# First MLP chunk by plain products, the activation sums of the seven-product scheme formed behind it, and the last modulation group in the merge

## The chip, the core and the metric

The kernel runs on one core of a Trainium2 chip. The metric is the device time of one launch in microseconds: the median of the runs. The kernel before takes 1075.11 us, the median of 3 runs from 1074.37 to 1075.24.

## What is computed

One trunk layer of a diffusion backbone, for 512 latent tokens and 128 context tokens, 640 in all, with 1024 features. A modulation vector comes from a product of the conditioning with `w_ada` (six groups of 1024 columns: shift, scale and gate for the mixer and for the MLP). The mixer joins two branches with sigmoid gates (called the merge here) and multiplies by `w_out`. Then comes the MLP, with a hidden width of 4096.

```python
shift1, scale1, gate1, shift2, scale2, gate2 = jnp.split(mod, N_MOD, axis=-1)
h = rmsnorm(x, pre1) * (1 + scale1) + shift1
mix = ((g_a * y_mlstm + g_b * y_attn) @ w_out)      # the merge, then the output product
x = x + gate1 * rmsnorm(mix, post1)
h = rmsnorm(x, pre2) * (1 + scale2) + shift2
ff = jnp.square(jax.nn.relu(h @ w_mlp1)) @ w_mlp2
x = x + gate2 * rmsnorm(ff, post2)
```

All of it is float32. A product of two float32 matrices is made of three products in a shorter format: each operand is split into a high and a low part, and high by high, high by low and low by high are summed (`mm3`, lines 116 to 118, or the inner loop of `product`, line 942).

## The kernel before

A TileContext takes the program in the order in which it is written, orders each engine's instructions with a simulated timeline (`schedule_with_timeline_sim`), and adds the waits. So an instruction written later can stand earlier on its engine where the simulation finds it ready. Within an engine the order is then fixed. `tc.issue_after(x)` puts the instructions of a block behind `x` on `x`'s engine.

**The merge** (lines 775 to 816) runs over eight blocks j of 128 features. Each takes 144 matmuls of 320 columns for two gates and two branch outputs. `ada_rest` (line 739) is a generator of eight modulation groups: each loads four pieces of `w_ada2` (512 KB each), makes one group of rows with 16 matmul instructions (`ada_rows`, line 149), and turns them with four transposes (line 155). One group is written ahead of the loop and one in each of j = 0 to 5. The eighth, cb = 7 (the second half of the MLP's gate), has a pool of its own (`own_pool`, line 737), is loaded through SP's queue and is written at line 980, after the output stage.

**The output stage** (lines 873 to 966) runs over five tiles of 128 tokens. `out_tile` has three parts: 48 matmuls of 512 columns into two banks; then the norm, the gate and the residual (the sum x2, line 895, which is also stored), and the second norm (lines 898 to 903); then eight transposes (line 907) into two banks and the modulation on ACT and VectorE (lines 911 and 914), which writes that tile's columns of `h2`. The transposes of tile t stand behind the matmuls of tile t+1. The eight `w_out` pieces take all eight units of the weight ring. PSUM is eight single banks here (line 921).

**The MLP** runs over eight chunks of 512 hidden columns, each made of two pairs of 256. A pair's product over 1024 features and 640 tokens is cut in two along hidden columns, features and tokens, and takes seven products in the place of eight, each of 12 matmuls of 320 columns. The seven need sums and differences of the activation's quarters, `S3` to `S7`, formed once from `h2` (lines 995 to 1018), and of the weights' quarters (`factors`, line 842: four subtractions on GpSimd, then high and low parts by `quarters` on ACT and VectorE). The quarters are `A(i, j)`, with tokens i and features j. `f2[1]` and `f2[2]` are the high and low parts of `A(0,0)` and `A(0,1)`, formed at tile 3 (lines 965 and 966). `squared` (line 1022) makes relu squared of each product and splits it. Then `sums` (line 1123) makes ten products of `w_mlp2`, 12 matmuls of 512 columns each, into `acc`, on chunk 0 with a copy (line 1140). `acc` takes the memory of `h2`.

In chunk 0 the two first products of each pair (`first_two`, line 947), which need `f2[1]` and `f2[2]` alone, are written ahead of the last tile's transposes. The other ten products of the two pairs alternate (line 1085), after `S3` to `S7`. `prime` (line 945) opens a bank with a product that counts for nothing, so that a copied partial sum can be added to.

Of the kernel before, what the change touches and what calls it, by code (L numbers as in the profile page):

```python
# [6 lines left out]
F32 = mybir.dt.float32  # L7
# [5 lines left out]
P = 128  # L13
NT = 5
TOK = 640
KD = 8
# [10 lines left out]
def _build(ctx, tc, nc, a, dbg):  # L27
# [44 lines left out]
    def bank2():  # L72
        return psum[2][1].tile([P, 1024], F32, name="b2")

    def bank1():
        return psum[1][1].tile([P, 512], F32, name="b1")
# [657 lines left out]
        pT.__exit__(None, None, None)  # L734
    dbg("aT", aT)

    own_pool = {}

    def ada_rest(pY):
        for cb in range(8):  # L740
            pY = own_pool.get(cb, pY)
            raws = []
            for u in range(4):
                raw = pY.tile([P, 2, 512], F32, name="aw2", bufs=3 if cb > 6 else 2)
                (nc.sync if cb > 6 else G).dma_start(raw, a["w_ada2"][cb * 4 + u].rearrange("p (k n) -> p k n", k=2))  # L745
# [27 lines left out]
    with pool("pY", side="right") as pY:  # L773
# [25 lines left out]
        for j in range(KD):  # L799
            sgs = []  # L800
            wy = [x.rearrange("p (q k n) -> p q k n", q=2, k=4) for x in load_w(a["w_y"][j])]
            for q in range(2):
                w = [x.rearrange("p (k n) -> p k n", k=8) for x in load_w(a["w_g"][q * 8 + j])]
                pg = halves(bank2())
                mode_b(pg, w, h1, KD)
                sg = pY.tile([P, TOK], F32, name=f"sg{q}", bufs=2)
                s3 = sg.rearrange("p (h n) -> p h n", h=2)
                S.activation(out=s3, in_=pg[:, :, 0:320], func=AF.Sigmoid)
                py = halves(bank2())
                mode_b(py, (wy[0][:, q], wy[1][:, q]), ys[q], 4)  # L810
                V.tensor_tensor(out=s3, in0=s3, in1=py[:, :, 0:320], op=ALU.mult)  # L811
                sgs.append(sg)
            V.tensor_tensor(out=sgs[0], in0=sgs[0], in1=sgs[1], op=ALU.add)
            S.copy(zh[:, j, :], sgs[0])
            V.tensor_tensor(out=zl[:, j, :], in0=sgs[0], in1=zh[:, j, :], op=ALU.subtract)
            next(ada, None) if j < 6 else None
    dbg("zh", zh); dbg("zl", zl)
    pO.__exit__(None, None, None)
    pN.__exit__(None, None, None)
# [53 lines left out]
    def out_tile(t):  # L873
# [28 lines left out]
        else:  # L902
            V.tensor_scalar(out=mix, in0=x2, scalar1=r, scalar2=None, op0=ALU.mult)
        yield
        pt = [bank1(), bank1()]
        for k in range(KD):
            mark["turn"] = T.transpose(pt[k // 4][:, k % 4 * 128:(k % 4 + 1) * 128], mix[:, k * 128:(k + 1) * 128], ident).ins
        for b in (1, 0):
            for k in range(4 * b, 4 * b + 4):
                if b:  # L910
                    S.activation(out=h2[:, k, c], in_=pt[1][:, k % 4 * 128:(k % 4 + 1) * 128], func=AF.Identity,
                                 scale=modA[1][:, k, gi:gi + 1], bias=modB[1][:, k, gi:gi + 1])
                else:
                    V.tensor_scalar(out=h2[:, k, c], in0=pt[0][:, k * 128:(k + 1) * 128], scalar1=modA[1][:, k, gi:gi + 1],
                                    scalar2=modB[1][:, k, gi:gi + 1], op0=ALU.mult, op1=ALU.add)
        yield

    weights(3, keep=1)
    pAd = pool("pAd", side="right")
    own_pool[7] = pAd.__enter__()  # L920
    banks(0, 8)
    wo = [tuple(x.rearrange("p (k n) -> p k n", k=2) for x in load_w(a["w_out"][u])) for u in range(8)]
    xs = {}

# [19 lines left out]

    def prime(b):
        T.matmul(b, f2[1][0][:, 0, 0:128], f2[1][0][:, 0, :], start=True, stop=True)
    def first_two(f, bX, bY):
        product(bX, f[1], f2[1], True)
        prime(bY)
        S.copy(bY, bX)  # L950
        product(bX, f[2], f2[2], False)

    behind = []
    for t in range(NT):
        if t >= 3:
# [6 lines left out]
        if t == 3:  # L962
            for j in range(2):
                f2[1 + j] = sub[:, 2 * j], sub[:, 2 * j + 1]
                S.copy(sub[:, 2 * j], A(0, j))
                V.tensor_tensor(out=sub[:, 2 * j + 1], in0=A(0, j), in1=sub[:, 2 * j], op=ALU.subtract)

    fs = [{}, {}]
    for n in range(2):
        raw = pW_.tile([P, 1024], F32, name="raw", bufs=2)  # L970
        nc.sync.dma_start(raw, a["w_mlp1"][2 * n])
        fs[n][1], fs[n][2] = quarters(raw)
    bs = [bank1()[:, 0:320] for _ in range(2)]
    first_two(fs[0], *bs)
    rests = [factors(*raw_pair(a["w_mlp1"][0:2]), fs[0])]
    bs += [bank1()[:, 0:320] for _ in range(2)]
    first_two(fs[1], *bs[2:])
    next(behind[-1])
    with tc.issue_after(mark["load"]):
        next(ada)  # L980
    next(ada, None)
    pZ.__exit__(None, None, None)
    pAd.__exit__(None, None, None)
    weights(0, keep=1)
    weights(1, keep=1)
    dbg("h2", h2)


# [3 lines left out]
    pH = pool("pH", side="left")  # L992
    pH_ = pH.__enter__()

    s1 = [pW_.tile([P, 1024], F32, name="raw", bufs=2)[:, 0:640].rearrange("p (k n) -> p k n", k=2) for _ in range(2)]
    ks = (slice(0, 2), slice(2, 4))
    fac = {i: [pH_.tile([P, 4, 320], F32R, name=f"S{i}" + s) for s in "hl"] for i in (3, 4, 7, 6, 5)}

# [2 lines left out]
        mark[f"S{i}"] = S.copy(hi, x).ins  # L1001
        V.tensor_tensor(out=lo, in0=x, in1=hi, op=ALU.subtract)

    for h, k in enumerate(ks):
        V.tensor_tensor(out=s1[h], in0=A(1, 0)[:, k, :], in1=A(1, 1)[:, k, :], op=ALU.add)
        parts(5, h, s1[h])
    for h, k in enumerate(ks):
        mark["S2"] = G.tensor_tensor(out=s1[h], in0=s1[h], in1=A(0, 0)[:, k, :], op=ALU.subtract).ins
        parts(6, h, s1[h])
    for h, k in enumerate(ks):  # L1010
        G.tensor_tensor(out=A(1, 0)[:, k, :], in0=A(0, 0)[:, k, :], in1=A(1, 0)[:, k, :], op=ALU.subtract)
        parts(7, h, A(1, 0)[:, k, :])
    for h, k in enumerate(ks):
        V.tensor_tensor(out=A(0, 1)[:, k, :], in0=A(0, 1)[:, k, :], in1=s1[h], op=ALU.subtract)
        parts(3, h, A(0, 1)[:, k, :])
    for h, k in enumerate(ks):
        parts(4, h, A(1, 1)[:, k, :])
    f2.update(fac)
    acc = pA_.tile([P, NT, 1024], F32, name="h1h")
    ssm = small.tile([P, NT, 4], F32, name="ssm", bufs=1)  # L1020

# [51 lines left out]
    for ch in range(NCH):  # L1073
        us = []
        if ch == 0:
            uu = [u_pair() for _ in range(2)]
            bs += [bank1()[:, 0:320] for _ in range(4)]
            for b in bs[6:]:
                prime(b)
# [5 lines left out]
            two = [pair(fs[i], True, uu[i], [bs[n] for n in b_]) for i, b_ in enumerate(((0, 4, 1, 6, 7), (2, 5, 3, 0, 4)))]  # L1085
            for i in (0, 0, 1, 0, 1, 0, 1, 0, 1, 1):
                next(two[i])
            us = [(u[0][n], u[1][n]) for u in uu for n in range(2)]
        else:
            if ch == 1:  # L1090
                banks(0, 5)
                pfork = tc.tile_pool(name="pfork", bufs=1, space=bass.MemoryType.PSUM, reuse_waits="tile")
                pfork_ = pfork.__enter__()
                forks = [pfork_.tile([P, 512], F32, name="b" + s)[:, 0:320] for s in "YWV"]

                for b in forks:
                    prime(b)
            for p in range(2):
                n = ch * 2 + p
                f = {}  # L1100
                factors(*raw_pair(a["w_mlp1"][2 * n:2 * n + 2]), f)()
# [4 lines left out]
        if ch == NCH - 1:  # L1106
# [7 lines left out]
        ws = [[load_w(a["w_mlp2"][ch, nh, m]) for m in range(2)] for nh in range(2)]  # L1114
# [149 lines left out]
```

## Time and profile before

| | us |
|---|---|
| median of the runs | 1075.11 |
| the profiled execution, its own time | 1075.53 |
| its span | 1073.6 |
| TensorE busy | 1025.3 |
| VectorE busy | 572.8 |
| ACT busy | 428.5 |
| GpSimd busy | 247.6 |
| last matmul of the output stage starts at | 612.01 |
| first product of chunk 1 starts at | 697.70 |

The table is read by stage: the merge ends at about 552 us, the output stage at 612 us, chunk 0 at 697 us, and seven more chunks follow. Matmuls overlap, so a matmul's own duration is longer than its share of the time. What counts is the distance from one start to the next.

### The profile page before, as it was taken

The numbers are of one execution on the slowest core, as the hardware profiler recorded it, in microseconds if no ns is written. First come the engines' busy times: TensorE is split into PE (matmuls) and PEld (weight loads), VectorE is DVE, ScalarE is ACT, GpSimd is POOL, SyncE is SP. The second block draws the span as 40 slices with busy tenths as digits, with TensorE's granted clock in tenths as the row PEclk, the third lists the DMA queues.
The fourth block names the chain that finished last, engine by engine and source line by source line (L and its number), as shares of the span: only waits on it lengthen the run. The fifth ranks groups of instructions, "written<-read, shape, count | busy, mean of one in ns | idle before, by whom it ended". The sixth has DMA issues, their size and how long they took to land.

```text
span 1073.6 us, 15721 instructions
## 1 busy us (share of the span) xinstructions
PE 1025.3 (96%) x6322; PEld 909.4 (85%) x6322; DVE 572.8 (53%) x963; ACT 428.5 (40%) x788; POOL 247.6 (23%) x222
## 2 busy tenths in 40 slices
PE   4999999899999999999999947999999999999997
PEld 2899899888789888888997837798989898989896
DVE  3655255577663223333343589465656566565557
ACT  4354243277775222222233554442424242424242
POOL 3011235424560000010000074222131314040201
PEclk9999999999999999999999977999999999999999
DMA  9444142111002444444355134222223131313034
GB/s 373 157 132 142 40 119 68 66 41 40 21 2 79 137 137 138 152 145 157 100 178 213 40 118 151 85 79 79 84 74 96 63 111 47 118 40 119 1 103 171
DMA packets 40408, 113.06 MB, mean 105 GB/s; under 512 B 4312, under 2 KB 14200, under 8 KB 39056
## 3 DMA queue, kind: packets, MB, share of 16 engines
q1 hardware_dynamic: 35520, 96.06, 26.4%
q0 software_dynamic: 4096, 14.70, 4.3%
q10 hardware_dynamic: 720, 1.31, 0.3%
q8 instruction: 49, 0.80, 0.3%
q14 instruction: 23, 0.19, 0.1%
HBM read 106.08 MB, written 5.98 MB: 104 GB/s over the span
## 4 chain that ended last, share of the span: by engine, by line
PE 89%; DVE 4%; POOL 2%; issue 2%; ACT 2%; DMA 1%; SPq 0%; POOLq 0%; DVEq 0%; ACTq 0%
PE b L116 19%; PE b L118 19%; PE b L117 19%; PE b L942 9%; PE bY L942 5%; PE b L149 3%; PE bV L942 2%; PE bW L942 2%; PE b L695 2%; PE b L229 2%; PE b L683 1%; PE b L470 1%; PE b L472 1%; PE b L496 1%; DMA x<-x 1%
## 5 line engine op out<-in xcount | busy, mean ns | idle before, releaser
L112 DVE TENSOR_TENSOR wl<-raw,wh 128x1024 fp32r<-128x1024 f32 (+2 forms) x64 | 77.7, 1215 | 163.3 <-ACT wh L111 163.3
L111 ACT CAST wh<-raw 128x1024 fp32r<-128x1024 f32 (+2 forms) x66 | 66.7, 1011 | 172.3 <-PE b L117 155.1
L117 PE MATMUL b<-h1l,wh 128*128 128x320 f32 x384 | 120.1, 313 | 0.0
L116 PE MATMUL b<-h1h,wh 128*128 128x320 f32 x384 | 119.8, 312 | 0.0
L118 PE MATMUL b<-h1h,wl 128*128 128x320 f32 x384 | 118.8, 309 | 0.0
L848 POOL TENSOR_TENSOR x<-gate 128x512 f32<-128x512 f32 x16 | 22.0, 1376 | 253.4 <-DMA gate<-w_mlp 250.4
L116 PEld LDWEIGHTS b<-h1h,wh 128*128 128x128 f32 x384 | 72.2, 188 | 6.3 <-DVE sg L811 4.2
L117 PEld LDWEIGHTS b<-h1l,wh 128*128 128x128 f32 x384 | 72.2, 188 | 6.0 <-issue 6.0
L118 PEld LDWEIGHTS b<-h1h,wl 128*128 128x128 f32 x384 | 72.2, 188 | 0.2 <-issue 0.2
L117 PE MATMUL b<-wlx,uh 128*128 128x512 f32 (+1 forms) x174 | 67.6, 389 | 0.0
L116 PE MATMUL b<-whx,uh 128*128 128x512 f32 (+1 forms) x174 | 66.9, 391 | 0.0
L1142 DVE TENSOR_TENSOR h1h<-h1h,b 128x512 f32<-128x512 f32 (+1 forms) x71 | 46.2, 672 | 37.0 <-PE b L118 36.8
L118 PE MATMUL b<-whx,ul 128*128 128x512 f32 (+1 forms) x174 | 64.3, 390 | 0.0
L117 PE MATMUL b<-wl,uh 128*128 128x512 f32 x150 | 59.1, 394 | 0.0
L1031 ACT CAST uh<-u 128x320 fp32r<-128x320 f32 x64 | 29.3, 459 | 72.6 <-DVE u L1028 41.5
L116 PE MATMUL b<-wh,uh 128*128 128x512 f32 x150 | 57.8, 396 | 0.0
L118 PE MATMUL b<-wh,ul 128*128 128x512 f32 x150 | 56.6, 395 | 0.0
L745 POOL DMA_DIRECT2D aw<-w_ada x28 | 15.2, 546 | 162.9 <-PE b L149 155.7
L612 POOL TENSOR_TENSOR pt<-pt,sm 128x640 f32<-128x640 f32 x32 | 40.0, 1255 | 46.9 <-DVE sm L610 44.6
L112 DVE TENSOR_TENSOR wlx<-raw,whx 128x1024 fp32r<-128x1024 f32 (+2 forms) x27 | 32.3, 1196 | 28.8 <-ACT whx L111 28.7
L149 PE MATMUL b<-aw,csil 128*32 128x256 f32 (+1 forms) x256 | 35.4, 526 | 9.1 <-DMA aw<-w_ada 9.1
L1032 DVE TENSOR_TENSOR ul<-u,uh 128x320 fp32r<-128x320 f32 x64 | 32.5, 509 | 13.6 <-ACT uh L1031 12.7
(443 smaller groups left out, 2852.8 us busy)
## 6 DMA issues: line engine op xcount, KB each, us to landing
raw<-w_mlp SPq DMA_DIRECT2D x34, 512.0 KB, 3.2
gate<-w_mlp SPq DMA_DIRECT2D x32, 512.0 KB, 4.7
aw<-w_ada POOLq DMA_DIRECT2D x28, 512.0 KB, 4.1
aw<-w_ada SPq DMA_DIRECT2D x8, 1024.0 KB, 12.0
raw<-w_g SPq DMA_DIRECT2D x16, 512.0 KB, 5.4
x<-x SPq DMA_DIRECT2D x10, 512.0 KB, 7.9
raw<-w_y SPq DMA_DIRECT2D x8, 512.0 KB, 3.4
raw<-w_out SPq DMA_DIRECT2D x8, 512.0 KB, 3.6
```

The source lines that it names most:

```text
L111: S.copy(hi, raw)
L112: eng.tensor_tensor(out=lo, in0=raw, in1=hi, op=ALU.subtract)
L116: T.matmul(out, lh, rh, start=start, stop=False)
L117: T.matmul(out, lh, rl, start=False, stop=False)
L118: T.matmul(out, ll, rh, start=False, stop=stop)
L149: T.matmul(ps[32 * j:32 * j + 32, 0:n], csil[:, k, :], raws[k], start=k < 4, stop=k >= 4, tile_position=(0, 32 * j))
L612: G.tensor_tensor(out=pt, in0=pt, in1=sm.broadcast_to([P, 640]), op=ALU.mult)
L848: G.tensor_tensor(out=t13[:, 0:512], in0=q2[0], in1=q1[0], op=ALU.subtract)
L942: T.matmul(out, w[u][:, k, :], x[v][:, k, :], start=start and k == 0 and i == 0, stop=k == 3 and i == 2, skip_group_check=True)
L1031: S.copy(uh[:, c], u)
L1032: V.tensor_tensor(out=ul[:, c], in0=u, in1=uh[:, c], op=ALU.subtract)
L1142: V.tensor_tensor(out=o, in0=o, in1=ps, op=ALU.add)
```

## The change

- The last modulation group goes back into the merge, at j = 6, through GpSimd's queue like the others, and its pool goes away.
- The output stage has four single banks and two double banks in the place of eight single ones; the transposes use the double ones.
- Chunk 0 multiplies four blocks of 128 hidden columns (`w0`, four loads) by both halves of the tokens, with 24 matmuls each. The first token half uses `f2[1]` and `f2[2]`, the second plain high and low parts of `A(1,0)` and `A(1,1)`, kept in the tiles `S3` and `S4`. The fourth block stands behind the last transposes on TensorE.
- `S5`, `S6`, `S7` and then the true `S3` are written behind these products. Their buffers `s1` are now those named `mix`.
- The extra weight unit comes at chunk 1, not ahead of chunk 0. Chunk 1's first factors stand behind the last `S2` subtraction on GpSimd, and chunk 0's `w_mlp2` pieces behind the last tile's modulation on ACT and VectorE.

```diff
-                raw = pY.tile([P, 2, 512], F32, name="aw2", bufs=3 if cb > 6 else 2)
-                (nc.sync if cb > 6 else G).dma_start(raw, a["w_ada2"][cb * 4 + u]...)
+                raw = pY.tile([P, 2, 512], F32, name="aw2", bufs=2)
+                G.dma_start(raw, a["w_ada2"][cb * 4 + u]...)
...
-            next(ada, None) if j < 6 else None
+            next(ada, None)
...
-        pt = [bank1(), bank1()]
+        pt = [bank2(), bank2()]
...
-    banks(0, 8)
+    banks(2, 4, (1, 2))
...
-    fs = [{}, {}]
-    for n in range(2):
-        raw = pW_.tile([P, 1024], F32, name="raw", bufs=2)
-        nc.sync.dma_start(raw, a["w_mlp1"][2 * n])
-        fs[n][1], fs[n][2] = quarters(raw)
-    bs = [bank1()[:, 0:320] for _ in range(2)]
-    first_two(fs[0], *bs)
-    rests = [factors(*raw_pair(a["w_mlp1"][0:2]), fs[0])]
-    bs += [bank1()[:, 0:320] for _ in range(2)]
-    first_two(fs[1], *bs[2:])
+    w0 = []
+    for m in range(4):
+        with tc.issue_after(mark["x2"]) if m == 3 else ExitStack():
+            w0.append([x.rearrange("p (k n) -> p k n", k=8) for x in load_w(a["w_mlp1"][m])])
+    pZ.__exit__(None, None, None)
+    weights(0, keep=1)
     next(behind[-1])
-    with tc.issue_after(mark["load"]):
-        next(ada)
-    next(ada, None)
...
+    for h in range(2):
+        parts(3, h, A(1, 0)[:, ks[h], :])
+    for h in range(2):
+        parts(4, h, A(1, 1)[:, ks[h], :])
...
         if ch == 0:
             uu = [u_pair() for _ in range(2)]
-            rests[0]()
-            with tc.issue_after(mark["S2"]), tc.issue_after(mark["S5"]):
-                rests.append(factors(*raw_pair(a["w_mlp1"][2:4]), fs[1]))
-            rests[1]()
-            two = [pair(fs[i], True, uu[i], ...) for i, b_ in enumerate(...)]
-            for i in (0, 0, 1, 0, 1, 0, 1, 0, 1, 1):
-                next(two[i])
             us = [(u[0][n], u[1][n]) for u in uu for n in range(2)]
+            for hf in range(2):
+                q = (f2[1], f2[2]) if hf == 0 else (f2[3], f2[4])
+                for m in range(CH):
+                    ps = bank1()[:, 0:320]
+                    with tc.issue_after(mark["turn"]) if m == 3 and hf == 0 else ExitStack():
+                        for k in range(KD):
+                            x = [y[:, k % 4, :] for y in q[k // 4]]
+                            mm3(ps, w0[m][0][:, k, :], w0[m][1][:, k, :], *x, k == 0, k == KD - 1)
+                    squared(*us[m], hf, ps=ps)
+            for h, k in enumerate(ks):                 # S5, S6, S7, true S3: moved here from ahead of chunk 0
+                V.tensor_tensor(out=s1[h], in0=A(1, 0)[:, k, :], in1=A(1, 1)[:, k, :], op=ALU.add)
+                parts(5, h, s1[h])
...
+            for h, k in enumerate(ks):
+                V.tensor_tensor(out=A(0, 1)[:, k, :], in0=A(0, 1)[:, k, :], in1=s1[h], op=ALU.subtract)
+                parts(3, h, A(0, 1)[:, k, :])
         else:
             if ch == 1:
+                weights(1, keep=1)
...
+                with tc.issue_after(mark["S2"]) if n == 2 else ExitStack():
+                    rest = factors(*raw_pair(a["w_mlp1"][2 * n:2 * n + 2]), f)
+                rest()
...
+        with tc.issue_after(mark["h2s"]) if ch == 0 else ExitStack(), tc.issue_after(mark["h2v"]) if ch == 0 else ExitStack():
+            ws = [[load_w(a["w_mlp2"][ch, nh, m]) for m in range(2)] for nh in range(2)]
```

## Rows read from the trace of the kernel before

**Rows 1.** The page: TensorE's busy tenths and its granted clock, in 40 equal slices.

```profile
PE   4999999899999999999999947999999999999997
PEclk9999999999999999999999977999999999999999
```

**Rows 2.** Busy time by stretch: length, PE, PEld, DVE, ACT, POOL, clock, DMA share.

```profile
622.00:635.00 13.00, 4.12 (x21) 1.25 (x20) 11.73 (x14) 8.00 (x14) 10.70 (x6) 0.75 0.48 159
635.00:656.00 21.00, 10.58 (x38) 9.29 (x39) 19.05 (x20) 7.61 (x11) 12.55 (x7) 0.59 0.17 59
656.00:697.80 41.80, 41.41 (x211) 35.51 (x210) 24.06 (x28) 19.42 (x32) 14.48 (x10) 1.00 0.35 122
697.80:750.50 52.70, 52.70 (x290) 47.23 (x289) 31.21 (x44) 18.40 (x30) 12.31 (x8) 1.00 0.25 80
```

**Rows 3.** TensorE's waits between 612 and 700 us: total, times, longest.

```profile
PE b L762 <- DVE gcol L758: 5.6, 1, 5.6
PE b L942 <- ACT wh L832: 5.0, 1, 5.0
PE b L942 <- DVE S6l L1002: 3.3, 1, 3.3
PE b L149 <- DMA aw<-w_ada: 2.8, 1, 2.8
```

**Rows 4.** TensorE's timeline: start, own duration, line, operands; idle before and its releaser.

```profile
575.94 1.09 PE L907 MATMUL b<-cst,mix 128*128 128x128 f32 x8 [1.82 <-ACT mix L901]
...
612.01 0.40 PE L118 MATMUL b<-whx,zl 128*128 128x512 f32 x1
612.62 1.09 PE L907 MATMUL b<-cst,mix 128*128 128x128 f32 x8 [0.21 <-ACT mix L901]
613.47 0.54 PE L942 MATMUL b<-h1l,whx 128*128 128x320 f32 x2
...
653.01 0.47 PE L942 MATMUL b<-S6h,wh 128*128 128x320 f32 x1
653.27 0.47 PE L942 MATMUL b<-S6l,wh 128*128 128x320 f32 x1
...
697.70 0.45 PE L942 MATMUL b<-h1l,wh 128*128 128x320 f32 x2
```

**Rows 5.** The chain that ended last, one product of chunk 1: start, length, what.

```profile
708.13 1.76 PE bY L942 x12
```

**Rows 6.** The merge blocks j = 6 and 7: length, TensorE busy, clock, DMA share, GB/s.

```profile
505.51:530.60 25.09, 25.09 (x166) 1.00 0.30 104
530.60:552.00 21.40, 21.40 (x147) 1.00 0.39 125
```

**Rows 7.** VectorE's timeline around the last tile and the sums, columns as in rows 4.

```profile
609.48 1.22 DVE L833 TENSOR_TENSOR wlx<-raw,whx 128x1024 fp32r<-128x1024 f32 x1
...
619.80 0.49 DVE L1028 TENSOR_TENSOR u<-u 128x320 f32<-128x320 f32 x1 [0.30 <-ACT u L1027]
620.21 0.75 DVE L903 TENSOR_SCALAR mix<-x,rs_x 128x1024 f32<-128x1024 f32 x1
...
626.34 3.70 DVE L1005 TENSOR_TENSOR raw<-h1h 128x640 f32<-128x640 f32 x2
...
642.35 3.69 DVE L1002 TENSOR_TENSOR S4l<-h1h,S4h 128x640 fp32r<-128x640 f32 x2
...
653.18 0.81 DVE L1002 TENSOR_TENSOR S3l<-h1h,S3h 128x640 fp32r<-128x640 f32 x1
```

**Rows 8.** GpSimd's timeline at the sums, columns as in rows 4.

```profile
629.32 4.59 POOL L1011 TENSOR_TENSOR h1h<-h1h 128x640 f32<-128x640 f32 x2
636.78 4.96 POOL L1008 TENSOR_TENSOR raw<-raw,h1h 128x640 f32<-128x640 f32 x2
641.71 1.84 POOL L848 TENSOR_TENSOR x<-gate 128x512 f32<-128x512 f32 x1
```

**Rows 9.** DMA issues of 590 to 700 us: count, KB each, median us to landing.

```profile
raw<-w_mlp SPq DMA_DIRECT2D x6, 512.0 KB, 3.3
```

More of the change, by code (lines that the diff above doesn't have):

```diff
@@ L735, in _build @@
     dbg("aT", aT)
-    own_pool = {}
     def ada_rest(pY):
         for cb in range(8):
-            pY = own_pool.get(cb, pY)
             raws = []
             for u in range(4):
-                raw = pY.tile([P, 2, 512], F32, name="aw2", bufs=3 if cb > 6 else 2)
-                (nc.sync if cb > 6 else G).dma_start(raw, a["w_ada2"][cb * 4 + u].rearrange("p (k n) -> p k n", k=2))
+                raw = pY.tile([P, 2, 512], F32, name="aw2", bufs=2)
+                G.dma_start(raw, a["w_ada2"][cb * 4 + u].rearrange("p (k n) -> p k n", k=2))
                 raws += [raw[:, 0, :], raw[:, 1, :]]
@@ L910, in out_tile @@
                 if b:
-                    S.activation(out=h2[:, k, c], in_=pt[1][:, k % 4 * 128:(k % 4 + 1) * 128], func=AF.Identity,
-                                 scale=modA[1][:, k, gi:gi + 1], bias=modB[1][:, k, gi:gi + 1])
-                else:
-                    V.tensor_scalar(out=h2[:, k, c], in0=pt[0][:, k * 128:(k + 1) * 128], scalar1=modA[1][:, k, gi:gi + 1],
-                                    scalar2=modB[1][:, k, gi:gi + 1], op0=ALU.mult, op1=ALU.add)
+                    mark["h2s"] = S.activation(out=h2[:, k, c], in_=pt[1][:, k % 4 * 128:(k % 4 + 1) * 128], func=AF.Identity,
+                                               scale=modA[1][:, k, gi:gi + 1], bias=modB[1][:, k, gi:gi + 1]).ins
+                else:
+                    mark["h2v"] = V.tensor_scalar(out=h2[:, k, c], in0=pt[0][:, k * 128:(k + 1) * 128], scalar1=modA[1][:, k, gi:gi + 1],
+                                                  scalar2=modB[1][:, k, gi:gi + 1], op0=ALU.mult, op1=ALU.add).ins
         yield
     weights(3, keep=1)
-    pAd = pool("pAd", side="right")
-    own_pool[7] = pAd.__enter__()
-    banks(0, 8)
+    banks(2, 4, (1, 2))
     wo = [tuple(x.rearrange("p (k n) -> p k n", k=2) for x in load_w(a["w_out"][u])) for u in range(8)]
@@ L946, in prime @@
         T.matmul(b, f2[1][0][:, 0, 0:128], f2[1][0][:, 0, :], start=True, stop=True)
[L947 to L951, printed above, removed]
     behind = []
@@ L993, in _build @@
     pH_ = pH.__enter__()
-    s1 = [pW_.tile([P, 1024], F32, name="raw", bufs=2)[:, 0:640].rearrange("p (k n) -> p k n", k=2) for _ in range(2)]
+    s1 = [pR_.tile([P, 1024], F32, name="mix", bufs=2)[:, 0:640].rearrange("p (k n) -> p k n", k=2) for _ in range(2)]
     ks = (slice(0, 2), slice(2, 4))
@@ L1002, in parts @@
         V.tensor_tensor(out=lo, in0=x, in1=hi, op=ALU.subtract)
[L1004 to L1017, printed above, removed]
     f2.update(fac)
+    for h in range(2):
+        parts(3, h, A(1, 0)[:, ks[h], :])
+    for h in range(2):
+        parts(4, h, A(1, 1)[:, ks[h], :])
     acc = pA_.tile([P, NT, 1024], F32, name="h1h")
@@ L1076, in _build @@
             uu = [u_pair() for _ in range(2)]
-            bs += [bank1()[:, 0:320] for _ in range(4)]
-            for b in bs[6:]:
-                prime(b)
-            rests[0]()
-            with tc.issue_after(mark["S2"]), tc.issue_after(mark["S5"]):
-                rests.append(factors(*raw_pair(a["w_mlp1"][2:4]), fs[1]))
-            rests[1]()
-            two = [pair(fs[i], True, uu[i], [bs[n] for n in b_]) for i, b_ in enumerate(((0, 4, 1, 6, 7), (2, 5, 3, 0, 4)))]
-            for i in (0, 0, 1, 0, 1, 0, 1, 0, 1, 1):
-                next(two[i])
-            us = [(u[0][n], u[1][n]) for u in uu for n in range(2)]
+            us = [(u[0][n], u[1][n]) for u in uu for n in range(2)]
+            for hf in range(2):
[11 more added lines that the diff above has]
+            for h, k in enumerate(ks):
+                mark["S2"] = G.tensor_tensor(out=s1[h], in0=s1[h], in1=A(0, 0)[:, k, :], op=ALU.subtract).ins
+                parts(6, h, s1[h])
+            for h, k in enumerate(ks):
+                G.tensor_tensor(out=A(1, 0)[:, k, :], in0=A(0, 0)[:, k, :], in1=A(1, 0)[:, k, :], op=ALU.subtract)
+                parts(7, h, A(1, 0)[:, k, :])
+            for h, k in enumerate(ks):
+                V.tensor_tensor(out=A(0, 1)[:, k, :], in0=A(0, 1)[:, k, :], in1=s1[h], op=ALU.subtract)
+                parts(3, h, A(0, 1)[:, k, :])
         else:
             if ch == 1:
+                weights(1, keep=1)
                 banks(0, 5)
@@ L1100, in _build @@
                 f = {}
-                factors(*raw_pair(a["w_mlp1"][2 * n:2 * n + 2]), f)()
+                with tc.issue_after(mark["S2"]) if n == 2 else ExitStack():
+                    rest = factors(*raw_pair(a["w_mlp1"][2 * n:2 * n + 2]), f)
+                rest()
                 u = u_pair()
@@ L1113, in _build @@
                 nc.sync.dma_start(x2[:, t, :], a["scratch_x2"][t])
-        ws = [[load_w(a["w_mlp2"][ch, nh, m]) for m in range(2)] for nh in range(2)]
+        with tc.issue_after(mark["h2s"]) if ch == 0 else ExitStack(), tc.issue_after(mark["h2v"]) if ch == 0 else ExitStack():
+            ws = [[load_w(a["w_mlp2"][ch, nh, m]) for m in range(2)] for nh in range(2)]
         last = ch == NCH - 1
```

4 lines of the change are left out of this document (removed).

## The prediction

> **What bounds the kernel now.** The page's slices come first: TensorE is at nine tenths or more almost everywhere, so a stage's time is its matmuls, and there is one hole, in two slices near 620 to 660 us, where the granted clock falls as well [rows 1]. The stretches give its size. From 622 to 656 us, 34.0 us, TensorE is busy for 14.7 and idle for 19.3 us, and its granted clock is 0.75 and then 0.59; the stretches behind are full at a clock of 1.00 [rows 2]. The waits say why: a modulation group's chain (5.6 us for `gcol`, 2.8 us for its last load), a weight factor (5.0 us) and the parts of an activation sum (3.3 us) [rows 3]. The timeline gives the ends: the last output matmul starts at 612.01, the first product of chunk 1 at 697.70 [rows 4].
>
> The hole is thus the work between `h2` and the products that need its sums. VectorE runs the first sum at 626.34 and the last split of the sums at 653.18 [rows 7], 27.6 us in all with that split, and in this time only a few products can run.
>
> **Prices.** Twelve matmuls of 320 columns take 1.76 us at the full clock [rows 5], 0.1467 us each. At 653 us starts are 0.26 us apart [rows 4], the lower of the two clocks, so a matmul then costs about 0.12 us more. A chunk in the steady state takes 52.70 us [rows 2], of which 14 x 1.76 = 24.64 are the seven-product part; the other 28.06 are 120 matmuls of 512 columns, 0.234 each. Eight transposes take 613.47 - 612.62 = 0.85 us [rows 4].
>
> **Chunk 0, before.** From the end of the output matmuls, 612.01 + 0.234 = 612.24, to 697.70 are 85.46 us [rows 4].
>
> **Chunk 0, after, with no wait added.** Tile 3's transposes with the wait ahead of them stay as they are: 613.47 - 612.24 = 1.23 us [rows 4]. Tile 4's add 0.85. The plain products are 4 blocks x 2 halves x 24 = 192 matmuls in the place of 168: 28.2 us, so the change pays 3.5 us in work. The `w_mlp2` part is 28.06 us. Three primes of chunk 1 are 0.44 us; the four others go, and lay in the hole. The sum is 58.8 us, 26.7 less than before.
>
> **The moved modulation group.** In the merge TensorE is full, so here it is paid in whole. A group written at the end of one block runs in the next. Block j = 6, which holds such a group, takes 25.09 us, and j = 7, which holds none, 21.40 [rows 6]: 3.7 us. By the matmuls of a block, 144 x 0.1467 = 21.1, it is 4.0, which I take. Its four loads leave SP's queue, where one stood behind the last `x2` store, and go to GpSimd's, as for the six groups before; in the block of [rows 6] that holds the last of those, TensorE was busy for 25.09 of 25.09 us, so I cost the queue at nothing. If that cover failed, a group would cost what its last load cost in the hole, 2.8 us [rows 3]. `gcol`, its transpose and the store of the gate row follow in the merge, and nobody needs them before the last chunk.
>
> So far the gain is 26.7 - 4.0 = 22.7 us.
>
> **Waits that the change may add**, none of them in the trace of before:
>
> - The third and fourth weight pieces. There are two raw buffers. The second is read until 609.48 + 1.22 = 610.7 [rows 7]; a load lands in 3.3 us [rows 9], cast and split take about 1.1 and 1.22, so a piece is there at about 616.5. The third block starts at 613.47 + 2 x 3.52 = 620.5. The fourth piece's split is ordered behind the `x2` sum, and queued on VectorE behind it is only the scaling of tile 4 at 620.21 [rows 7], while its block starts at 625. Between 0 and 1.2 us (one split late): 0.6.
> - The plain `S3` and `S4`. Tile 4's scaling ends at 620.96 [rows 7], so its transposes fit behind the third block, at 624.0, and end at 624.9. Modulation (some 1.4 us, as in the timeline of the four operations) and one cast of 0.7 and one split of 0.81 [rows 7] put the first parts at about 628; the first half's fourth block ends at 628.4. The four splits in a row end at about 631, and `S4` is first read at 630.2. With two squares of 0.49 + 0.49 [rows 7] and a weight split ahead of them it would be 4 us later. Between 0 and 4: 1.0.
> - `acc` over `h2`. The products end at 628.4 + 14.1 + about 1 = 643.5. `acc` may not be written before the last sum is formed from `h2`; with four banks, four of the ten sums, 2.81 us each, can run without it, until 654.7. The chain from 629 needs 27.6 us if it is as slow as before, so 656.6: 1.9 us late. But before it shared its engines with two pairs' factors; with splits at 0.81 us and nothing between, it ends near 646, when TensorE leaves the old `S3`. The far end is in the rivals. Between 0 and 1.9 here: 0.8.
> - Chunk 1's factors: two units of weights come free only late in chunk 0's `w_mlp2` part, after its seventh sum, about 8 us ahead of chunk 1, and two casts and two splits of about 1.1 and 1.22 each follow. Between 0 and 2.8 (as if one load were late): 0.3.
>
> Together 2.7 us. A wait of this size does not move the clock here: after the 1.82 us ahead of tile 0's transposes [rows 4] the slices stay at nine tenths or more [rows 1].
>
> **Weight against the trace.** The sums move to a time when GpSimd forms chunk 1's factors. Beside GpSimd a VectorE split took 1.85 us (`S4l`), and without it 0.81 (`S3l`) [rows 7]. In the Trainium skill, "SBUF — State Buffer", section "Who interferes with whom", only the port pair that VectorE and GpSimd share causes contention, as an exclusive lock; a VectorE instruction with two SBUF inputs contends with a GpSimd one that reads SBUF. The slow split agrees with it; that it would make GpSimd's and VectorE's times add up here is the first rival, and the time would be 1066.
>
> **The rivals.**
>
> 1. *The sums come late.* VectorE's work from 625: 16 sums and splits of 0.81, eight squares of 0.98, four weight splits of 1.22, 1.4 of modulation: 27 us, to 652. GpSimd's: 4.96 + 4.59 + four factor steps of 1.84 [rows 8] = 16.9. If each instruction holds the other engine up, the chain ends near 669 and TensorE waits 14 us for `acc`; half of that is likelier, since in 635 to 656 us the two were busy for 19.05 + 12.55 in 21.0 us [rows 2]. Time: 1058.5 to 1067.
> 2. *Tile 4's transposes stand too early on TensorE.* They are written ahead of the plain products, and only the fourth block is bound to stand behind them. If the simulated order puts them first, TensorE idles from 613.5 to 621.0: 7.5 us, and some 25 matmuls at the lower clock cost 3 more. Time: about 1066. Against it: before, VectorE took chunk 0's square at 619.80, ahead of tile 4's scaling that is written earlier [rows 7], so the order follows readiness.
> 3. *Slower.* If the order on VectorE puts the sums behind the second half's squares, chunk 0's `w_mlp2` splits and chunk 1's factors, the chain begins at 644, plus seven weight splits of 1.22, and at 27.6 us ends at 680; TensorE waits for `acc` from 654.7, 25 us, and comes back at the lower clock, some 40 matmuls at 0.12 = 4.8. That is 30 + 1.9 against 22.7: about 1085. It decides from a chain that ends after 671. For it speaks that GpSimd and ACT steps of the chain wait for each other; against it the same row of readiness [rows 7].
> 4. *The change does not do what it says: the hole only moves*, to the second half's start, which waits for the plain `S3` and `S4` as the sums' products waited before. To eat the gain that wait must be about 22 us, so ACT and VectorE would have to take other work first. Against it: the last columns of `h2` are there when the first sum starts, at 626.34 [rows 7], and the weight splits that could come ahead are seven of 1.22 us. Time: about 1075.
>
> **How the numbers follow.** 1075.53 - 22.7 + 2.7 = 1055.5 for the profiled execution; the median of the runs is 0.4 lower, so 1055.1. Its own range, from no wait to all the bounds above, is 1052.4 to 1059. Chances: forecast 0.62, late sums 0.21, early transposes 0.08, no change 0.02, slower 0.07. The range takes in the first three up to 1066. About 0.2% is what a measurement of this kernel can tell from no change. Faster 0.91, same 0.02, slower 0.07.
>
> **What would show it.** Right: the slices have no hole and a full clock; merge block j = 7 is some 4 us longer and j = 6 unchanged; from the last output matmul to chunk 1 about 61.5 us; no wait over 2 us there; `S3l` written for the second time before the fifth sum of chunk 0. Wrong: a wait of the fifth sum for ACT's copy into `acc`, transposes ahead of the third block with idle time in front, a fall of the granted clock, or a steady chunk that is no longer 52.7 us.

## The result, and the profile after

| | before | after |
|---|---|---|
| median of the runs, us | 1074.98 | 1057.12 |
| lowest to highest of four runs, us | 1074.37 to 1075.24 | 1055.42 to 1059.04 |
| the profiled execution, its own time, us | 1075.53 | 1055.42 |
| its span, us | 1073.6 | 1053.7 |

The ratio of the times is 0.9835, with a 95% interval from 0.9818 to 0.9853: 17.9 us faster by the medians, 1.65%. The forecast was 1055.1 with a range from 1052 to 1066. The median before is of four runs here; the 1075.11 us ahead of the prediction were of three of them. The profiled execution was the fastest of its four, 20.1 us faster than the profiled execution before.

The page's slices of the kernel after: TensorE's busy tenths and granted clock. The hole of [rows 1] is gone, and one slice in its place is at eight tenths.

```profile
PE   4999999899999999999999998999999999999997
PEclk9999999999999999999999999999999999999999
```

Chunk 0, from the end of the output matmuls to the first product of chunk 1, in the kernel before and in the kernel after, and then chunk 1 after (length, then busy time of PE, PEld, DVE, ACT, POOL, then clock, DMA share, GB/s). The first line:

```profile
612.24:697.70 85.46, 65.56 (x333) 54.97 (x333) 61.09 (x72) 40.64 (x70) 38.70 (x25) 0.86 0.33 111
```

and the kernel after:

```profile
612.15:677.57 65.42, 60.80 (x333) 53.55 (x332) 45.48 (x59) 35.89 (x62) 26.06 (x15) 0.97 0.27 89
...
677.73:730.40 52.67, 52.67 (x290) 47.21 (x290) 31.66 (x44) 18.84 (x31) 12.64 (x9) 1.00 0.30 100
```

Chunk 0 is 20.0 us shorter, and the steady chunk is the same as in [rows 2]. TensorE's waits from 500 to 720 us after (total, times, longest), in the place of [rows 3]:

```profile
PE b L117 <- DVE wlx L112: 2.4, 1, 2.4
PE b L116 <- ACT u L995: 1.6, 1, 1.6
PE b L117 <- DVE S3l L979: 0.4, 1, 0.4
PE b L904 <- DVE mix L900: 0.2, 1, 0.2
```

The timeline of TensorE after (start, own duration, what; idle before it), in the place of [rows 4]:

```profile
612.15 0.46 PE L116 MATMUL b<-h1l,whx 128*128 128x320 f32 x2
...
617.15 1.04 PE L904 MATMUL b<-cst,mix 128*128 128x128 f32 x8
...
624.01 1.06 PE L904 MATMUL b<-cst,mix 128*128 128x128 f32 x8 [0.25 <-DVE mix L900]
...
628.87 0.45 PE L116 MATMUL b<-S3h,whx 128*128 128x320 f32 x2
629.89 0.41 PE L117 MATMUL b<-S3l,whx 128*128 128x320 f32 x1 [0.42 <-DVE S3l L979]
...
649.20 0.50 PE L117 MATMUL b<-wlx,uh 128*128 128x512 f32 x1 [2.37 <-DVE wlx L112]
...
650.72 0.63 PE L116 MATMUL b<-whx,uh 128*128 128x512 f32 x1
651.15 0.63 PE L117 MATMUL b<-wlx,uh 128*128 128x512 f32 x1
...
655.06 0.50 PE L116 MATMUL b<-whx,uh 128*128 128x512 f32 x1 [1.58 <-ACT u L995]
...
677.57 0.46 PE L937 MATMUL b<-h1l,wh 128*128 128x320 f32 x2
```

The reader sees the plan at work: plain products from 612.15, both groups of transposes between them, tile 4's at 624.01 with 0.25 us of idle time, and the second half on `S3` from 628.87, 4 us after the fourth block began. The hole is closed up to 646.8 us. There the products with `w_mlp2` wait for the low part of a weight piece (`wlx`) until 649.20. From 650.3, 1.1 us behind this wait, starts are 0.43 us apart in the place of 0.234, the lower clock (1.2 GHz), and ahead of 655.06 TensorE waits for a bank that a square (line 995) has still to read.

### The profile page after: what moved, and what is told of

Its sections match the earlier page's. It is cut to its first block, busy times and chain, and to the rows that moved or that the text cites. A ratio compares the mean times of both kernels' runs of the same rounds, so it can differ in the third digit from the quotient of the medians.

```text
span 1053.7 us, 15728 instructions
## 1 busy us (share of the span) xinstructions
PE 1022.7 (97%) x6342; PEld 907.0 (86%) x6342; DVE 561.0 (53%) x955; ACT 424.2 (40%) x784; POOL 238.1 (23%) x218
## 4 chain that ended last, share of the span: by engine, by line
PE 89%; DVE 5%; ACT 2%; issue 2%; DMA 1%; POOL 1%; SPq 0%; POOLq 0%; DVEq 0%; ACTq 0%
PE b L116 20%; PE b L117 20%; PE b L118 20%; PE b L937 7%; PE bY L937 5%; PE b L149 3%; PE bV L937 2%; PE bW L937 2%; PE b L695 2%; PE b L683 2%; PE b L229 1%; PE b L496 1%; PE b L470 1%; DMA x<-x 1%; DMA gate<-w_mlp 1%
## 5 line engine op out<-in xcount | busy, mean ns | idle before, releaser
L112 DVE TENSOR_TENSOR wl<-raw,wh 128x1024 fp32r<-128x1024 f32 (+2 forms) x67 | 80.5, 1202 | 157.7 <-ACT wh L111 156.4
L111 ACT CAST wh<-raw 128x1024 fp32r<-128x1024 f32 (+2 forms) x69 | 69.8, 1013 | 175.0 <-PE b L117 157.0
L117 PE MATMUL b<-h1l,wh 128*128 128x320 f32 x400 | 125.2, 313 | 0.0
L117 PEld LDWEIGHTS b<-h1l,wh 128*128 128x128 f32 x400 | 75.2, 188 | 6.9 <-issue 6.9
L117 PE MATMUL b<-wlx,uh 128*128 128x512 f32 (+1 forms) x164 | 64.5, 393 | 2.4 <-DVE wlx L112 2.4
L116 PE MATMUL b<-whx,uh 128*128 128x512 f32 (+1 forms) x164 | 64.1, 395 | 1.6 <-ACT u L995 1.6
L117 PE MATMUL b<-wl,uh 128*128 128x512 f32 x160 | 63.2, 395 | 0.0
L116 PE MATMUL b<-wh,uh 128*128 128x512 f32 x160 | 62.1, 396 | 0.0
L118 PE MATMUL b<-whx,ul 128*128 128x512 f32 (+1 forms) x164 | 61.5, 393 | 0.0
L118 PE MATMUL b<-wh,ul 128*128 128x512 f32 x160 | 60.4, 394 | 0.0
L117 PEld LDWEIGHTS b<-wlx,uh 128*128 128x128 f32 x164 | 31.1, 190 | 9.6 <-DVE wlx L112 2.8
```

Source lines behind the costliest of these rows:

```text
L111: S.copy(hi, raw)
L112: eng.tensor_tensor(out=lo, in0=raw, in1=hi, op=ALU.subtract)
L116: T.matmul(out, lh, rh, start=start, stop=False)
L117: T.matmul(out, lh, rl, start=False, stop=False)
L118: T.matmul(out, ll, rh, start=False, stop=stop)
```

## Experiments

Times are medians of four runs (three rounds and the profile) unless another number stands beside them. "Chunk 0" is the stretch above, read from each trace; it is free of what the first part of the kernel does. The runs are of several chips, on which the kernel before had medians from 1074.98 to 1076.27 us, so a difference of about 1 us between two medians tells nothing unless they are said to be of one chip. Chunk 0 repeats better: 65.42, 65.46 and 65.66 us in three profiles in which VectorE has the same order.

**What holds up chunk 0: take the sums away.** The edit drops the four loops over `S5`, `S6`, `S7` and the true `S3`, and with them the mark that chunk 1's factors stand behind:

```diff
+    f2[5], f2[6], f2[7] = fac[3], fac[4], fac[3]
...
-            for h, k in enumerate(ks):
-                V.tensor_tensor(out=s1[h], in0=A(1, 0)[:, k, :], in1=A(1, 1)[:, k, :], op=ALU.add)
-                parts(5, h, s1[h])
...
-                with tc.issue_after(mark["S2"]) if n == 2 else ExitStack():
+                with ExitStack():
```

> The changed kernel without the sums: the steps that form S5, S6, S7 and the true S3 are left out, and chunks 1 to 7 multiply by S3 and S4 in their place, so these chunks' values differ. Theory: the 7.0 us that chunk 0 waits (65.4 us from the first plain product to chunk 1, against 58.4 of matmuls and transposes) come from the sums, which fill VectorE's queue from 626 to 654 us. Without them the stretch is 59 to 60 us, no wait over 1 us, and the time falls by 5.5 to 6.5 us, to about 1051 by the median. Rival: the second w_mlp2 piece is late because of its raw buffer and its load; then a wait of about 2 us ahead of the third group of sums over w_mlp2 stays, and the gain is under 4 us.

Measured: 1057.69 us, no gain; chunk 0 took 65.86 us. Both expectations missed. The waits of 2.4 and 1.6 us were gone as the theory had it, but a new one had come ahead of tile 4's transposes. TensorE's waits, and GpSimd's timeline in that place:

```profile
PE b L904 <- DVE mix L900: 5.5, 1, 5.5
```

```profile
625.82 1.27 POOL L845 TENSOR_TENSOR x<-gate 128x512 f32<-128x512 f32 x1 [7.32 <-DMA gate<-w_mlp]
627.05 1.70 POOL L846 TENSOR_TENSOR x<-gate 128x512 f32<-128x512 f32 x1
628.72 0.79 POOL L100 TENSOR_TENSOR rs_x<-ms,mhalf 128x1 f32<-128x1 f32 x1
```

The one small step of tile 4's norm that runs on GpSimd (`rs_x`, line 100) stands behind two factor steps of chunk 1, which wait for their load. The experiment had taken two things away, the sums and an order on GpSimd. The second had to be put back.

**The same, with chunk 1's first weight blocks loaded late:**

```diff
-                with ExitStack():
+                with tc.issue_after(sent[0].ins) if n == 2 else ExitStack():
                     rest = factors(*raw_pair(a["w_mlp1"][2 * n:2 * n + 2]), f)
```

> The kernel without the sums again (S5, S6, S7 and the true S3 are left out, chunks 1 to 7 multiply by S3 and S4 in their place, so their values differ), now with chunk 1's first weight blocks loaded late, since without the sums their factor steps had come early and held up tile 4's norm for 5.5 us. It is the floor of chunk 0: theory 59 to 60 us, no wait over 1 us, time about 6 us below the changed kernel. Rival: waits of 2 us or more stay that have nothing to do with the sums or the factors.

Measured: 1051.83 us, 5.3 below the changed kernel. The stretches of chunk 0:

```profile
612.89:672.53 59.64, 58.82 (x332) 52.85 (x331) 33.74 (x47) 30.56 (x54) 14.79 (x11) 1.00 0.29 98
```

So 59.6 us is the floor of chunk 0 (with a wait of 0.7 us ahead of tile 4's transposes), and 5.8 of the 65.4 us come with the sums and the factors beside them. The time of the whole, on another chip than the changed kernel's, fell about as expected.

**Write the `w_mlp2` pieces ahead of the sums.** The four `load_w` of chunk 0's `w_mlp2` move up, ahead of the loop for `S5`.

> The changed kernel with chunk 0's four w_mlp2 pieces written ahead of the sums, so that their splits come earlier on VectorE. Theory: the wait of 2.4 us for the piece's low part goes, with it the lower clock behind it (1.5 us); the sums come some 5 us later, to about 659, and TensorE, which may not write acc until then, has four banks: a wait for the bank of 1 to 4 us stays. Gain 1 to 4 us. Rival: squares and sums only change places on VectorE, and the time stays within 1 us.

Measured: 1056.44 us, chunk 0 in 65.46 us, the same waits (2.4 and 1.5 us); the expected gain did not come. VectorE's timeline there has the same steps in the same order as in the changed kernel. Presumably what is written earlier was no more ready in the simulated timeline; this is not shown. Since the edit moved nothing, it decides nothing between the causes.

**Move GpSimd's factor steps away from the sums.** In the changed kernel VectorE (first fence) and GpSimd (second) work side by side from 636 to 648 us:

```profile
636.13 3.53 DVE L979 TENSOR_TENSOR S7l<-h1h,S7h 128x640 fp32r<-128x640 f32 x2 [2.21 <-ACT S7h L978]
639.58 2.20 DVE L1065 TENSOR_TENSOR h1h<-h1h,mix 128x640 f32<-128x640 f32 x1
641.70 1.58 DVE L1000 TENSOR_TENSOR ul<-u,uh 128x320 fp32r<-128x320 f32 x1
643.20 1.91 DVE L979 TENSOR_TENSOR S6l<-mix,S6h 128x640 fp32r<-128x640 f32 x1
645.04 1.91 DVE L1065 TENSOR_TENSOR h1h<-h1h,mix 128x640 f32<-128x640 f32 x1
646.87 2.28 DVE L112 TENSOR_TENSOR wlx<-raw,whx 128x1024 fp32r<-128x1024 f32 x1
```

```profile
636.83 4.27 POOL L1059 TENSOR_TENSOR mix<-mix,h1h 128x640 f32<-128x640 f32 x2
641.06 1.88 POOL L845 TENSOR_TENSOR x<-gate 128x512 f32<-128x512 f32 x1
642.89 1.54 POOL L846 TENSOR_TENSOR x<-gate 128x512 f32<-128x512 f32 x1
644.39 1.88 POOL L848 TENSOR_TENSOR x<-gate,x 128x512 f32<-128x512 f32 x1
646.34 1.73 POOL L849 TENSOR_TENSOR x<-gate,x 128x512 f32<-128x512 f32 x1
```

The edit loads chunk 1's first weight blocks behind chunk 0's last `w_mlp2` piece, and leaves the order on TensorE and GpSimd as it is:

```diff
-                with tc.issue_after(mark["S2"]) if n == 2 else ExitStack():
+                with tc.issue_after(mark["S2"]) if n == 2 else ExitStack(), tc.issue_after(sent[0].ins) if n == 2 else ExitStack():
```

> The changed kernel with chunk 1's first pair of weight blocks loaded behind chunk 0's last w_mlp2 piece on SP's queue, so that GpSimd's four factor steps (641 to 648 us in the changed kernel) come after the sums; nothing else changes its order but two small VectorE and ACT steps. Theory: VectorE steps beside GpSimd are slow (S6l 1.91 us against 0.81, the w_mlp2 split 2.28 against 1.22), and this makes the split late that TensorE waits for. From 641 on four steps lose 4 to 5 us: the wait of 2.4 us goes, the lower clock with it, the wait of 1.6 us falls. Time: 3 to 5 us less, chunk 0 in 60.5 to 62.5 us in the place of 65.4. Rival: VectorE's work itself is too much, contention or not: under 1.5 us less; or the factors are now late for chunk 1 and a wait at 678 us takes the gain back.

Measured: 1054.22 us, 2.9 below the changed kernel by the medians; chunk 0 took 61.56 us, 3.9 less. VectorE's timeline with the late factors:

```profile
642.41 2.20 DVE L1065 TENSOR_TENSOR h1h<-h1h,mix 128x640 f32<-128x640 f32 x1
644.53 0.48 DVE L1000 TENSOR_TENSOR ul<-u,uh 128x320 fp32r<-128x320 f32 x1
644.93 0.81 DVE L979 TENSOR_TENSOR S6l<-mix,S6h 128x640 fp32r<-128x640 f32 x1
645.67 0.81 DVE L1065 TENSOR_TENSOR h1h<-h1h,mix 128x640 f32<-128x640 f32 x1
646.40 1.21 DVE L112 TENSOR_TENSOR wlx<-raw,whx 128x1024 fp32r<-128x1024 f32 x1
```

The same four steps, in the same order, are 1.1 us shorter each, and the wait of 2.4 us for `wlx` is gone, with the lower clock behind it. The theory's size for the stretch held (60.5 to 62.5 us); the time, 3 to 5 us less by the theory, came out just short of it by medians of different chips.

**The sums all on VectorE, factors late.** The two subtractions of `S6` and `S7` change their engine, `G.tensor_tensor` to `V.tensor_tensor`, on top of the last edit.

> As the kernel with the late factors, and the four subtractions that GpSimd makes for S6 and S7 on VectorE as well, so that GpSimd is idle while the sums are formed. Theory: VectorE takes four steps of 0.8 us more, and loses the slow ones beside GpSimd (S7l 1.77 against 0.81, twice; the true S3's first sum 2.2 against 0.8) and the time in which it waits for GpSimd (2.2 us at 634). The sums end 6 us earlier than in the changed kernel, no wait over 1 us is left in chunk 0, stretch 59 to 60.5 us, time 5 to 6 us below the changed kernel, about 1051.5. Rival: the added steps stand ahead of the squares and of the w_mlp2 split, and a wait of 2 us or more stays.

Measured: 1052.67 us, chunk 0 in 60.33 us; the true `S3` is finished at 648.4 in the place of 654.2.

```profile
613.99:674.32 60.33, 58.98 (x333) 52.66 (x331) 44.24 (x63) 36.27 (x64) 16.39 (x11) 1.00 0.27 97
```

The stretch went as expected, within 0.7 us of the floor, and no wait is over 0.7 us. The time is 4.5 us below the changed kernel's where 5 to 6 were expected. The stretch is 1.2 us shorter than with the late factors alone: VectorE with four steps more is faster here than VectorE and GpSimd side by side.

**The sums on VectorE, factors where they were.**

> The changed kernel with the S6 and S7 subtractions on VectorE and the factors as they are. GpSimd's factor steps now come beside the sums. Theory: contention stays with the factor steps but GpSimd's 11 us of sums are gone, so about half of the gain of the kernel that has both: 2 to 4 us. Rival: the factor steps start earlier and slow VectorE's steps at 626 to 636, ahead of the plain S3 and S4: the time is the same or up to 3 us more.

Measured: 1058.07 us, chunk 0 in 66.58 us. The rival's mechanism, early factors, was right, and its size, but not its place: the mark is now VectorE's, so nothing holds the factors back on GpSimd, and `rs_x` came at 628.38 in the place of 622.35. TensorE waited 5.5 us for tile 4's `mix`, as without the sums.

```profile
626.90 1.50 POOL L846 TENSOR_TENSOR x<-gate 128x512 f32<-128x512 f32 x1
628.38 0.54 POOL L100 TENSOR_TENSOR rs_x<-ms,mhalf 128x1 f32<-128x1 f32 x1
```

**Both versions on one chip.**

> The changed kernel unaltered, once more, for the spread of its first part and as the neighbour of the other runs here. Expected: 1055.5 to 1059, chunk 0 again 65.4 us with waits of 2.4 and 1.6 us, and the start of the merge within 2.6 us of the ten profiles so far.

> The kernel with the sums all on VectorE and the late factors, beside the changed kernel on one chip. If the first result holds: 4 to 6 us faster than the changed kernel in the same call, 1051.5 to 1053.5, chunk 0 in 60.3 us. Rival: the difference to the changed kernel was one between chips, and is under 2 us here.

Measured: 1057.21 us (1056.17 to 1060.34; a little above the expected end) and 1053.28 us (1052.95 to 1053.79); chunk 0 in 65.66 and 60.72 us. The version with the sums on VectorE and late factors is 3.9 us faster than the changed kernel, just short of the 4 to 6 expected, and so not a difference between chips. It beats both the kernel before and the changed kernel: its ratio to the kernel before is 0.9798, interval 0.9784 to 0.9813.

**The modulation group alone.** The kernel before, with the last group in the merge and its pool away:

```diff
-            next(ada, None) if j < 6 else None
+            next(ada, None)
...
-    with tc.issue_after(mark["load"]):
-        next(ada)
-    next(ada, None)
```

> The kernel before with the last modulation group moved to the merge and nothing else. Theory: the merge pays 4.0 us; the hole loses the waits for gcol and for the group's load (5.6 + 2.8 us) only as far as the sums do not set its end. The sums were in VectorE's queue from 626.3 and GpSimd's from 629.3, and the group's steps stood between them: about 3 us shorter. So the time is 1075 to 1078, no gain from this part. Rival: the group was what held the hole open, and the time falls by 4 us or more, to under 1071.

Measured: 1076.74 us (ten runs), ratio to the kernel before 1.0018, interval 1.0006 to 1.0029. The stretch from the first product behind the output stage to chunk 1 fell by 2.8 us, from 84.23 to 81.46, the merge grew by 4.0. TensorE's waits from 612 to 700 us:

```profile
PE b L937 <- DVE S6l L993: 8.8, 1, 8.8
PE b L937 <- DVE S5l L993: 6.4, 1, 6.4
PE b L937 <- ACT S5h L992: 6.3, 1, 6.3
```

The waits for `gcol` and for the load [rows 3] are gone, and longer ones for the sums stand there. So the group had only stood in a hole that the sums held open, and its move alone gains nothing, as expected.

**The changed kernel with the group as before**, late and with its own pool:

> The changed kernel with the last modulation group as in the kernel before: own pool, loads on SP's queue, written behind the last transposes. Theory: the merge loses 4.1 us, and chunk 0, which is full, pays about 4 us and, by the row reduction and its copies on VectorE and ACT, 0 to 3 more: the time is 0 to 3 us above the changed kernel's, 1057 to 1060. Rival: chunk 0 waits 7 us anyway and takes the group into that wait: then the time is 3 to 4 us below, about 1053.

Measured: 1058.16 us, 1.0 above the changed kernel. Chunk 0 took 70.67 us, 5.25 more, against the 4 us by which the merge is shorter. Once the hole is closed the group finds no room there. Whether this 1.0 us is there can't be told from the spread of 3 us of either kernel's runs.

**All first-half blocks behind the last transposes:**

```diff
-                    with tc.issue_after(mark["turn"]) if m == 3 and hf == 0 else ExitStack():
+                    with tc.issue_after(mark["turn"]) if hf == 0 else ExitStack():
```

> The changed kernel with all four blocks of the first token half bound to stand behind the last tile's transposes on TensorE. Theory: in the changed kernel the blocks fill the 11 to 12 us between the last output matmul (612.15) and the last transposes (624.01). Bound behind them, TensorE waits for tile 4's norm, some 8 to 9 us, the granted clock falls, and matmuls behind it cost 0.12 us more each for a while: 8 to 13 us slower than the changed kernel, 1065 to 1070. Rival: the sums and the w_mlp2 split then come relatively earlier, the waits of 2.4 and 1.6 us vanish, and the loss is under 6 us.

Measured: 1062.84 us, 5.6 above the changed kernel on the same chip. TensorE waited 7.08 us ahead of tile 4's transposes and 2.87 ahead of tile 3's, and the transposes themselves ran at the lower clock (1.97 us for eight, 1.06 above). The waits of 2.4 and 1.6 us were gone. So the rival had it, and the loss of 8 to 13 us did not come: part of it is given back.

```profile
617.74 1.27 PE L904 MATMUL b<-cst,mix 128*128 128x128 f32 x8 [2.87 <-ACT mix L898]
626.09 1.97 PE L904 MATMUL b<-cst,mix 128*128 128x128 f32 x8 [7.08 <-DVE mix L900]
```

**Eight single banks again:**

```diff
-        pt = [bank2(), bank2()]
+        pt = [bank1(), bank1()]
...
-    banks(2, 4, (1, 2))
+    banks(0, 8)
```

> The changed kernel with the eight single PSUM banks of the kernel before in the output stage and chunk 0. Theory: the output stage was 2.0 us shorter in the changed kernel (last zh cast to the first plain product 56.7 us, 58.7 before) because with four single banks tile 0's transposes were put behind tile 1 and part of tile 2, and with eight directly behind tile 1, where TensorE waits 1.8 us. So the wait of 1.8 us comes back; in chunk 0 eight banks take the wait of 1.6 us for a square away. Time: within 1.5 us of the changed kernel. Rival: the banks do not set this order, and the output stage stays at 56.7 us.

Measured: 1064.68 us, 7.5 above the changed kernel; both expectations missed. In the output stage the wait ahead of tile 0's transposes came back, as the theory had said, but here the lower clock followed it, and the stage took 60.3 us, 3.6 more than in the changed kernel.

```profile
578.85 1.84 PE L904 MATMUL b<-cst,mix 128*128 128x128 f32 x8 [1.81 <-ACT mix L898]
...
626.57 1.97 PE L904 MATMUL b<-cst,mix 128*128 128x128 f32 x8 [7.26 <-DVE mix L900]
```

But tile 4's transposes now stand directly behind tile 3's, ahead of the first three blocks, and TensorE waits 7.26 us for them. Chunk 0 takes 70.0 us, 4.4 more than the 65.66 of the changed kernel on this chip. This is the second rival of the prediction. The shape of PSUM decided between it and the forecast.

## Why the prediction was right, and where it was not

- **The main term holds.** Plain products need only high and low parts of `h2`, and the sums' chain lies beside 192 plain matmuls and the `w_mlp2` part. By the predicted sum chunk 0 without waits is 58.8 us, of which 0.4 was the idle time ahead of tile 3's transposes; the floor without sums is 59.6.
- **The moved group holds.** The merge's casts of `zh`, first and last start, tell its price: 381.7 to 553.6 before, 379.6 to 555.5 after, so 171.9 and 175.9, 4.0 us more. The two lines are of the kernel before and of the kernel after, in that order:

```profile
L814 ACT CAST zh<-sg x8: 717/730/731, 381.7 to 553.6; 128x640 fp32r<-128x640 f32 x8
```

```profile
L811 ACT CAST zh<-sg x8: 721/730/732, 379.6 to 555.5; 128x640 fp32r<-128x640 f32 x8
```

- **The waits were mis-sized: 2.7 us forecast, 6.6 by the stretch** (65.4 where 61.5 were forecast). Of the four that were listed, the weight pieces of the first half cost nothing, `S3` 0.4, `acc` over `h2` no wait of its own, chunk 1's factors none. The two that came were left out of the list: the second `w_mlp2` piece, and a bank that a square had still to read. The unit for the piece is free by 637.6 at the latest, when the plain products have read the last of such units (`whx`). Its cast then stands on ACT behind the cast of `S6h`, which waits for GpSimd:

```profile
639.01 0.73 ACT L978 CAST S6h<-mix 128x640 fp32r<-128x640 f32 x1 [1.02 <-POOL mix L1059]
639.65 1.04 ACT L111 CAST whx<-raw 128x1024 fp32r<-128x1024 f32 x1
```

From there its split stood behind 7 us of slowed VectorE steps, up to 646.87. 2.4 us of wait, some 1.6 us of lower clock behind it, 1.6 us for the square's bank, 0.4 for `S3` and 0.25 ahead of tile 4's transposes make 6.2 of the 6.6.

- **The first rival was right in its mechanism and wrong in its place.** Steps beside GpSimd took 1.9 us where they take 0.81 alone, and moving GpSimd's steps gave 3.9 us of the stretch back. But the one who waited was the weight split, not `acc`. The rule that was weighed there, the exclusive lock of "SBUF — State Buffer", "Who interferes with whom", in the Trainium skill, fits both traces: the same step took 1.91 us beside GpSimd and 0.81 without it. The two engines' times nearly add up. From 641.06 to 649.07, 8.0 us, GpSimd made four factor steps, and one such step takes 1.29 us where VectorE is idle:

```profile
684.00 1.29 POOL L845 TENSOR_TENSOR x<-gate 128x512 f32<-128x512 f32 x1 [10.01 <-DMA gate<-w_mlp]
```

VectorE made four steps that take 0.48, 0.81, 0.81 and 1.21 us alone. One after the other that is 5.2 + 3.3 = 8.5 us. Busy time does not tell this, since a slowed step counts as busy for all its length: from 636 to 649 us VectorE was busy for 12.76 and GpSimd for 11.99 of 13.0 us. For the same reason the rival's sum was too long: its 1.84 us for a factor step was already a slowed one.

- **"A wait of this size does not move the clock here" was wrong.** The 1.82 us of [rows 4] left it at the upper level. The wait of 2.37 us from 646.8 was followed, 1.1 us after its end, by eight matmuls at the lower one (granted clock 0.50):

```profile
650.30:653.20 2.90, 2.90 (x8) 1.98 (x6) 2.90 (x5) 1.88 (x3) 0.00 (x0) 0.50 0.75 223
```

- **A gain that was not forecast, and a spread, cover the miss.** The output stage, from the last cast of `zh` to the end of its matmuls, was 58.7 us before and 56.7 after: the changed banks moved tile 0's transposes, and the wait of 1.82 us [rows 4] went. The prediction had cost the banks at nothing. The run with eight banks shows what they are worth to the changed kernel: 7.5 us by the medians, and in the traces 3.6 in that stage and 4.4 in chunk 0, by the place of tile 4's transposes. And the profiled execution reached the merge 2.1 us earlier than the one before, though nothing ahead of the merge is changed; this is no gain but the spread below. Without it the profiled time is 1057.5, near the median of 1057.1.
- **The sum for the profiled execution:** 2.1 us less up to the merge, 4.0 more in it, 2.0 less in the output stage, 20.0 less in chunk 0 and 0.2 more behind: 19.9 less in the span, where 20.0 were forecast. The right total is partly luck: 3.9 us too little wait, 2.0 of a gain not seen, and 2.1 of spread. By the medians 17.9 of the 20.0 us came.
- **Its range and its signs.** The bounds of the four waits add up to 9.9 us, so "from no wait to all the bounds" ends at 1062.3, not at 1059. And two of its own signs went against it: there was a wait over 2 us in chunk 0, and the granted clock fell.
- **The other rivals.** Early transposes were a real case: chunk 0 took 6.0 us more when they were forced (71.7 us) and 4.4 with eight banks. The 10.5 us that the rival reckoned was too much, since waits behind them are given back. The hole did not move to the second half's start, which waited 0.4 us. The slower case did not come near: the chain's last split ended at 654.3 us, not after 671.

## What to carry to other kernels

A hole that is filled with work to hide a chain of preparations is better closed by work that needs no preparation, even if it costs some matmuls more: here 3.5 us more of products, with the banks that leave tile 4's transposes behind them and the group out of the way, took 20 us off chunk 0. When a chain is moved beside other work, count the queue of every engine that it passes through, and who is queued behind it; two engines that slow each other to half speed can be slower than one of them alone. And where a scheduler orders by readiness, a new shape of PSUM or a lost ordering mark changes the order of steps that the edit never names: the order on each engine is the first thing to compare.

## What the runs showed of the hardware that was not expected

- VectorE steps with two SBUF inputs ran at 0.81 us (640 elements), 1.21 (1024) and 0.48 (320) alone, and at 1.91, 2.28 and 1.58 beside GpSimd steps: about 1.1 us more each in this stretch. A step of 512 elements took 0.68 us alone and 1.29 at 663.07 beside GpSimd, only 0.6 more.
- The same instructions ahead of the merge took different times from run to run: the first cast of `zh` started between 379.6 and 382.8 us in fourteen profiles of kernels that are alike up to there. A difference of 3 us between two single profiles of this kernel says nothing.
- A wait of 1.8 us ahead of tile 0's transposes left TensorE's clock at the upper level in the kernel before [rows 4] (granted clock 1.00 from 575.94 to 577, 1.09 us for eight transposes). With eight banks it was followed by the lower level (0.56 from 578.85, 0.50 from 580.34 to 582.20; 1.84 us for eight transposes). So the length of a wait alone did not decide.
